# Half of the conv taps on ScalarE and GpSimd, pair sums of four heads at once, one-hot groups of 16 tokens, gate matmuls with a PSUM stride of four

## The chip, the core and the metric

The kernel runs on one core of a Trainium2 chip. Its engines have one instruction queue each and take their instructions in order: TensorE (PE, with its weight loads shown apart as PEld), VectorE (DVE), ScalarE (ACT), GpSimd (POOL) and SyncE (SP), which starts most of the transfers. They wait for one another by semaphores. The metric is the device time in microseconds, the median of the runs.

## The reference, cut to what matters

One layer with 512 tokens of width 1024. A norm and one input projection feed two groups: a conv module and differential attention with four heads. Both results are concatenated and projected out. Then each token picks experts: eight heads, each with two sets of 128 keys, of which the 16 best pairs are taken.

```python
def conv_module(cv, cg, w, b, ln_g, ln_b):
    u = cv * jax.nn.sigmoid(cg)
    y = lax.conv_general_dilated(u, w[:, None, :], window_strides=(1,),
        padding=[(CONV_KERNEL - 1, 0)], feature_group_count=CONV_WIDTH) + b   # 31 taps per channel
    return jax.nn.silu(layer_norm(y, ln_g, ln_b))

# expert choice, per token and head
sv, si = lax.top_k(s, 16)                                   # s: 8 heads x 2 x 128 key scores
cand = sv[:, :, 0, :, None] + sv[:, :, 1, None, :]
cs, ci = lax.top_k(cand.reshape(T, 8, 256), 16)
e1 = take_along_axis(si[:, :, 0], ci // 16); e2 = take_along_axis(si[:, :, 1], ci % 16)
gates = softmax(cs)
# h = gelu(x . u_tab[e1 * 128 + e2]) * gate;  y = sum of h * v_tab[e1 * 128 + e2]
```

## The kernel before

The program is one list of tile operations. A scheduler turns it into one fixed queue per engine before the run, with the waits in it; long work without a deadline (the conv taps) is set between other work of its engine. Every large product is made in three passes on PE, from a high and a low part of both operands: `split` lets ACT write the high part (`whi`, `uhi`, line 62 or 583) and DVE or POOL the remainder (`wlo` on DVE, line 63; `qlo` on POOL, line 603; `ulo` on POOL or DVE, line 584).

The stages, by the trace's times:

- To 201 us, the front. PE runs the input projections, 128 rows of weights at a time (`whi`, `wlo`), then attention in units of one head and one query tile. From a head's raw queries and keys (`qraw`, line 230 on ACT) DVE makes the rotated ones (lines 234 to 241); ACT takes the exponentials (`p`, line 257), DVE mixes the two maps (line 267). POOL takes the small rsqrt steps of three heads (lines 80 to 83, 128x4). The gated input of the conv `u` is four tiles of 128 channels and 512 tokens with 30 more columns in front. ACT writes the first tap of each (line 363), and DVE adds 30 more per tile, each one multiply and add of 128x512 (line 365, `cy<-u,convw,cy`), 120 in all. They stand between DVE's other work from 46 to 198 us. Behind them come the conv's norm and its Silu.
- 201 to 256 us: output projection, residual and second norm.
- 256 to 398 us: routing. For each head and key set a query projection, scores for three tiles of 128 tokens (TA = 384 of the 512), and `top16`, five DVE operations (lines 495 to 499). `pairs` (lines 504 to 512) adds the sorted scores of one head and one token tile, 64 and 48 candidates, and takes the `top16` of them.
- 398 to 444 us: the last of it, and the decoding of the first token tile (lines 514 on).
- 444 to 646 us: the gate stage. For each of three token tiles the choice is turned into a dense matrix of gates over 128 x 128 experts. A group of GB = 8 tokens takes a one-hot matrix `o1` of the first index and `eq` of the second (128x1024 f16 each, tokens in pairs), two products of `eq` with the high and the low part of the gates (`o`, lines 651 and 652), and for each token two matmuls that write 128 columns of a PSUM bank (line 658). ACT copies a bank with four tokens to `stage` (line 660). DVE makes `o1` (line 646), except for every third group of four, where ACT does, by eight `Abs` of 128x128 and a `Relu` (lines 640 and 642). Between the groups stand up-projections of the experts (`up`, lines 577 to 594): a load, `uhi` on ACT, `ulo` on POOL for the first 40 of them, 24 matmuls and a Gelu.
- 664 us to the end: the rest of the experts, where PE multiplies nearly without a gap, and for the last 128 tokens rows are gathered instead.

Of the kernel before, what the change touches and what calls it, by code (L numbers as in the profile page):

```python
# [34 lines left out]
GB = 8  # L35
# [5 lines left out]
FIRST, STEP = 12, 2  # L41
ACT_EVERY = 3
# [11 lines left out]
def hymba_layer(ctx: ExitStack, tc: tile.TileContext, I, out):  # L54
# [3 lines left out]
    def load(dst, src):  # L58
        nc.sync.dma_start(dst, src)
# [33 lines left out]
    # ---------------------------------------------------------------- front  # L93
# [18 lines left out]
    # the tensor engine's clock comes up, and the first table, while the first loads are on their way  # L112
# [51 lines left out]
    # 1 / rms of every token, as a column per token tile and along the free axis of all partitions  # L164
# [33 lines left out]
    lams = cload("lams", [128, 4, HD], I["lams"].to_broadcast([128, 4, HD]))  # L198
# [44 lines left out]
    # attention in units of (head, query tile), three stages apart  # L243
# [65 lines left out]
    # the layer's own embedding, projected  # L309
# [76 lines left out]
    # ------------------------------------------------- output projection, second norm  # L386
# [75 lines left out]
    # ------------------------------------------------- expert routing  # L462
# [22 lines left out]
    ne1 = rt.tile([128, NA, 128], F32, name="ne1")  # L485
# [5 lines left out]
    A.activation(irep, iota[:, :, None].to_broadcast([128, 128, 2]), AF.Copy)  # L491

# [60 lines left out]
    def decodeA(t):  # L553
# [4 lines left out]
        A.activation(ne1[:, t], tp[:, 0:128], AF.Copy, scale=-1.0)  # L558
# [37 lines left out]
    for h in range(NH):  # L596
# [18 lines left out]
        for t in range(NA):  # L615
            pairs(setA, t, h)
# [296 lines left out]
```

## Time and profile before

| | us |
|---|---|
| median of 3 runs | 1631.94 (1630.68 to 1632.47) |
| span of the profiled execution | 1628.7 |
| PE busy in the span | 1538.4 (94%) |
| PE weight loads | 1334.0 (82%) |
| DVE busy | 1296.2 (80%) |
| ACT busy | 706.2 (43%) |
| POOL busy | 537.4 (33%) |

The profiled execution's span is 3.2 us below the median. The granted clock of TensorE is 0.974 of full speed over the span. A share of the whole span is a mean over the stages above; which engine sets the end of a stage is read from the stage alone. The time of a row is that of one instruction with its own latency, so a row's mean is larger than the distance from start to start where instructions follow closely.

### The profile page before, as it was taken

The page shows a single profiled execution, that of the slowest core. Times are in us where ns is not written, and L with a number is a line of the kernel's source. Part 1 is how long each engine was busy: PE and PEld are TensorE (multiplying, and loading weights), DVE is VectorE, ACT ScalarE, POOL GpSimd, SP SyncE. Part 2 cuts the span into 40 slices and gives each one's busy share as a digit, 9 for nine tenths or more (in the row PEclk, how much of TensorE's full clock was granted, in tenths as well). Part 3 has the DMA queues.
Part 4 walks back from the last instruction along what each step waited for, and adds up shares of the span by engine and source line. Part 5 has one row for each costly group of instructions (what it writes and reads, how often), then busy time and mean ns, then how long its engine had stood idle before and what let it go on. Part 6 is the DMA issues. An engine that isn't in the chain of part 4 may idle for free. (4 is left out here: it accounts for less than half of the span.)

```text
span 1628.7 us, 22295 instructions
## 1 busy us (share of the span) xinstructions
PE 1538.4 (94%) x7945; PEld 1334.0 (82%) x7945; DVE 1296.2 (80%) x2564; ACT 706.2 (43%) x1116; POOL 537.4 (33%) x360
## 2 busy tenths in 40 slices
PE   8999898999688887999999999999999999999997
PEld 6866576888577776988888889999999999997886
DVE  4999875988989998478887888777777777777657
ACT  5434643322488796433333333333333333324432
POOL 1000103442353342244444444444444444430000
PEclk9999998999899998999999999999999999999999
DMA  7210254221234645989999999988988899977612
GB/s 241 93 66 33 74 188 154 93 85 40 78 148 169 241 179 227 316 302 355 330 351 319 347 336 351 328 325 315 330 319 319 325 320 334 328 256 258 211 44 78
DMA packets 147648, 374.83 MB, mean 230 GB/s; under 512 B 12113, under 2 KB 66129, under 8 KB 146001
## 3 DMA queue, kind: packets, MB, share of 16 engines
q1 hardware_dynamic: 110672, 239.18, 42.3%
q0 software_dynamic: 36864, 134.23, 21.9%
q8 instruction: 62, 1.02, 0.2%
q14 instruction: 50, 0.40, 0.1%
HBM read 338.76 MB, written 34.60 MB: 229 GB/s over the span
## 5 line engine op out<-in xcount | busy, mean ns | idle before, releaser
L66 PE MATMUL ups<-mTH,uhi 128*128 128x384 f32 x1024 | 354.9, 347 | 4.0 <-ACT ga L594 4.0
L68 PE MATMUL ups<-mTH,ulo 128*128 128x384 f32 x1024 | 352.9, 345 | 5.6 <-POOL ulo L584 5.6
L67 PE MATMUL ups<-mTL,uhi 128*128 128x384 f32 x1024 | 351.2, 343 | 0.0
L583 ACT ACTIVATE uhi<-uraw 128x1024 fp32r<-128x1024 f32 x128 | 135.6, 1061 | 278.6 <-PE ups L67 251.5
L718 POOL DMA_INDIRECT row<-in_u,bidx x128 | 180.1, 1407 | 224.2 <-DVE scr L722 211.4
L718 POOL DMA_INDIRECT row<-in_v,bidx x128 | 182.6, 1427 | 206.8 <-DVE acc L730 189.4
L709 PE MATMUL y<-vlo,hH 128*128 128x512 f32 x768 | 238.5, 392 | 2.0 <-DVE vlo L63 2.0
L709 PE MATMUL y<-vhi,hH 128*128 128x512 f32 x768 | 239.0, 392 | 0.3 <-ACT vhi L62 0.3
L709 PE MATMUL y<-vhi,hL 128*128 128x512 f32 x768 | 239.0, 392 | 0.0
L66 PEld LDWEIGHTS ups<-mTH,uhi 128*128 128x128 f32 x1024 | 196.6, 192 | 8.6 <-ACT ga L594 4.6
L68 PEld LDWEIGHTS ups<-mTH,ulo 128*128 128x128 f32 x1024 | 196.1, 192 | 7.0 <-POOL ulo L584 6.9
L67 PEld LDWEIGHTS ups<-mTL,uhi 128*128 128x128 f32 x1024 | 196.0, 191 | 4.9
L62 ACT ACTIVATE hH<-hf 128x384 fp32r<-128x384 f32 x128 | 67.0, 524 | 285.2 <-issue 219.3
L63 DVE TENSOR_TENSOR hL<-hf,hH 128x384 fp32r<-128x384 f32 x128 | 71.2, 557 | 146.0 <-ACT hH L62 145.8
L584 POOL TENSOR_TENSOR ulo<-uraw,uhi 128x1024 fp32r<-128x1024 f32 x40 | 123.4, 3090 | 177.3 <-ACT uhi L583 155.6
L709 PEld LDWEIGHTS y<-vlo,hH 128*128 128x128 f32 x768 | 144.0, 188 | 35.4 <-DVE vlo L63 4.0
L709 PEld LDWEIGHTS y<-vhi,hL 128*128 128x128 f32 x768 | 144.2, 188 | 31.3 <-DVE rsq L73 0.2
L722 DVE SCALAR_TENSOR_TENSOR scr<-row,mB 128x1024 f32<-128x1024 f32 x128 | 156.1, 1220 | 15.4 <-DMA row<-in_u,bidx 15.4
L709 PEld LDWEIGHTS y<-vhi,hH 128*128 128x128 f32 x768 | 143.1, 188 | 25.4 <-ACT vhi L62 1.0
L730 DVE SCALAR_TENSOR_TENSOR acc<-row,bh,acc 128x1024 f32<-128x1024 f32 x127 | 162.5, 1279 | 0.0
L63 DVE TENSOR_TENSOR vlo<-vraw,vhi 128x1024 fp32r<-128x1024 f32 x128 | 156.1, 1220 | 0.8 <-ACT vhi L62 0.8
L584 DVE TENSOR_TENSOR ulo<-uraw,uhi 128x1024 fp32r<-128x1024 f32 x88 | 107.5, 1221 | 37.2 <-ACT uhi L583 37.1
(277 smaller groups left out, 2447.9 us busy)
## 6 DMA issues: line engine op xcount, KB each, us to landing
uraw<-in_ut SPq DMA_DIRECT2D x128, 512.0 KB, 6.1
vraw<-in_v SPq DMA_DIRECT2D x128, 512.0 KB, 4.7
g_spill<-stage SPq DMA_DIRECT2D x12, 2048.0 KB, 6.9
gt<-g_spill SPq DMA_DIRECT2D x32, 768.0 KB, 9.7
qraw<-in_wq SPq DMA_DIRECT2D x16, 512.0 KB, 3.6
wraw<-in_w_in SPq DMA_DIRECT2D x15, 512.0 KB, 3.9
woraw<-in_w_out SPq DMA_DIRECT2D x8, 512.0 KB, 4.2
et<-in_wg SPq DMA_DIRECT2D x8, 512.0 KB, 4.3
```

What stands on the lines that cost most here:

```text
L62: A.activation(hi, src, AF.Copy)
L63: V.tensor_tensor(lo, src, f32(hi), op=OP.subtract)
L66: T.matmul(ps, wh, xh, start=first, stop=False)
L67: T.matmul(ps, wh, xl, start=False, stop=False)
L68: T.matmul(ps, wl, xh, start=False, stop=last)
L583: A.activation(hi, raw, AF.Copy)
L584: (P if c in first else V).tensor_tensor(lo, raw, f32(hi), op=OP.subtract)
L709: T.matmul(y[t][n], w[:, sl], x[:, n * 512:n * 512 + 512], start=c == 0 and w is hH and x is hi, stop=c == NK - 1 and l)
L718: P.indirect_dma_start(out=row, out_offset=None, in_=I["u"] if i < 128 else I["v"], in_offset=bass.IndirectOffsetOnAxis(ap=bidx[:, j:j + 1 ...
L722: tc.keep_in_program_order(V.scalar_tensor_tensor(scr, row, 1.0, mB, op0=OP.mult, op1=OP.mult, accum_out=ba[:, j:j + 1]))
L730: tc.keep_in_program_order(V.scalar_tensor_tensor(acc, row, bh[:, j:j + 1], acc, op0=OP.mult, op1=OP.add))
```

## The change

Four edits.

- Conv: the tiles are taken in the order 2, 3, 0, 1. For tiles 2 and 3 each of the 30 taps is an ACT scaling into `tap` (two buffers) and a POOL addition `cy += tap`. Tiles 0 and 1 stay on DVE.
- `pairs` is called once for four heads (HG = 4), after the fourth: two additions over four heads, 128x4x64 and 128x4x4x12, then the `top16` of each head.
- The one-hot groups have 16 tokens (GB = 16), so DVE's operations are 128x2048. Every second group has its `o1` made by a POOL subtraction, then `Abs` and `Relu` on ACT over 128x2048 each. The number of up-projections per token stays (STEP = 1).
- The gate matmuls write every fourth column of their PSUM bank (`gb[:, j::4]`), so that ACT reads the bank in order and writes runs of four elements.

```diff
-GB = 8
+GB = 16
+HG = 4
+POOL_CT = 2
-FIRST, STEP = 12, 2
-ACT_EVERY = 3
+FIRST, STEP = 12, 1
+ACT_EVERY = 2
...
-    lams = cload("lams", [128, 4, HD], I["lams"].to_broadcast([128, 4, HD]))
+    lams = inp.tile([128, S], F32, name="qraw", bufs=2)[:, 0:4 * HD].rearrange("p (a d) -> p a d", a=4)
+    load(lams, I["lams"].to_broadcast([128, 4, HD]))
...
-    for ct in range(4):
+    for ct in (2, 3, 0, 1):
         A.activation(cy[:, ct], u[:, ct, 0:S], AF.Identity, scale=convw[:, ct, 0:1], bias=convb[:, ct:ct + 1])
         for j in range(1, TAPS):
-            V.scalar_tensor_tensor(cy[:, ct], u[:, ct, j:j + S], convw[:, ct, j:j + 1], cy[:, ct], op0=OP.mult, op1=OP.add)
+            if ct < 4 - POOL_CT:
+                V.scalar_tensor_tensor(cy[:, ct], u[:, ct, j:j + S], convw[:, ct, j:j + 1], cy[:, ct], op0=OP.mult, op1=OP.add)
+            else:
+                tap = mid.tile([128, S], F32, name="tap", bufs=2)
+                A.activation(tap, u[:, ct, j:j + S], AF.Copy, scale=convw[:, ct, j:j + 1])
+                P.tensor_tensor(cy[:, ct], cy[:, ct], tap, op=OP.add)
...
-        cand = rbp.tile([128, NCAND], F32, name="cand", bufs=2)
-        V.tensor_tensor(cand[:, 0:NC0].rearrange("p (a b) -> p a b", a=4), sv[:, t, h, 0, 0:4][:, :, None].to_broadcast([128, 4, TOPK]),
-                        sv[:, t, h, 1][:, None, :].to_broadcast([128, 4, TOPK]), op=OP.add)
...
-        top16(cand, cs[:, t, h], ci[:, t, h], NCAND)
+        hs = slice(h, h + HG)
+        cand = rbp.tile([128, HG, NCAND], F32, name="cand")
+        V.tensor_tensor(cand[:, :, 0:NC0].rearrange("p h (a b) -> p h a b", a=4), sv[:, t, hs, 0, 0:4][:, :, :, None].to_broadcast([128, HG, 4, TOPK]),
+                        sv[:, t, hs, 1][:, :, None, :].to_broadcast([128, HG, 4, TOPK]), op=OP.add)
...
+        for j in range(HG):
+            top16(cand[:, j], cs[:, t, h + j], ci[:, t, h + j], NCAND)
...
-        for t in range(NA):
-            pairs(setA, t, h)
+        if h % HG == HG - 1:
+            for t in range(NA):
+                pairs(setA, t, h + 1 - HG)
...
-                if g % ACT_EVERY == ACT_EVERY - 1:
-                    ab = gst.tile([128, GB, 128], F16, name="ab", bufs=1)
-                    for j in range(GB):
-                        A.activation(ab[:, j], iota, AF.Abs, bias=ne1[:, t, tk + j:tk + j + 1])
-                    o1 = gst.tile([128, GB, 128], F16, name="o1a", bufs=1)
-                    A.activation(o1, ab, AF.Relu, bias=ones[:, 0:1], scale=-1.0)
+                if (tk // GB + t * (128 // GB)) % ACT_EVERY == ACT_EVERY - 1:
+                    o1 = gst.tile([128, GB, 128], F16, name="o1", bufs=2)
+                    P.tensor_tensor(o1, iota16[:, None, :].to_broadcast([128, GB, 128]),
+                                    e1T[:, t, tk:tk + GB][:, :, None].to_broadcast([128, GB, 128]), op=OP.subtract)
+                    A.activation(o1, o1, AF.Abs)
+                    A.activation(o1, o1, AF.Relu, bias=ones[:, 0:1], scale=-1.0)
...
-                            T.matmul(gb[:, j * 128:j * 128 + 128], o2[:, i, jj // 2, :, jj % 2], pick1[jj], start=i == 0, stop=i == 1)
+                            T.matmul(gb[:, j::4], o2[:, i, jj // 2, :, jj % 2], pick1[jj], start=i == 0, stop=i == 1)
                     t0 = g * GB + 4 * q
-                    A.activation(stage[:, :, t0:t0 + 4].rearrange("p e t -> p t e"),
-                                 gb.rearrange("p (t e) -> p t e", t=4), AF.Copy, scale=1.0 / GS)
+                    A.activation(stage[:, :, t0:t0 + 4], gb.rearrange("p (e t) -> p e t", t=4), AF.Copy, scale=1.0 / GS)
```

The lines move: in the changed program ACT's scaling is line 372, POOL's addition 373, a DVE tap 369, the exponential 260, POOL's one-hot subtraction 651, `ulo` 595, `qlo` 614.

ACT's queue before the change, from the last projections of the front to the first exponential of attention (`p`, line 257). `whi` is the high part of a weight tile, `qraw` a head's queries or keys:

```order
L62 ACTIVATE whi<-wraw 128x1024
L230 ACTIVATE qraw<-bank 128x512
L62 ACTIVATE whi<-wraw 128x1024
L230 ACTIVATE qraw<-bank 128x512
L62 ACTIVATE whi<-wraw 128x1024
L230 ACTIVATE qraw<-bank 128x512
L257 ACT_TABLE_LOAD
L257 ACTIVATE p_809,zz<-bank,nm 128x128
```

The same stretch after the change:

```order
L372 ACTIVATE tap<-u,convw 128x512 x6
L64 ACTIVATE whi<-wraw 128x1024
L233 ACTIVATE qraw<-bank 128x512
L372 ACTIVATE tap<-u,convw 128x512 x8
L233 ACTIVATE qraw<-bank 128x512
L64 ACTIVATE whi<-wraw 128x1024
L372 ACTIVATE tap<-u,convw 128x512 x8
L233 ACTIVATE qraw<-bank 128x512
L64 ACTIVATE whi<-wraw 128x1024
L372 ACTIVATE tap<-u,convw 128x512 x6
L64 ACTIVATE whi<-wraw 128x1024
L233 ACTIVATE qraw<-bank 128x512
```

Behind the last row of it stands the same table load and exponential: all 60 scalings come ahead of it. In POOL's queue the 60 additions are one row, directly ahead of the first rsqrt step.

POOL's queue before, from the last query projections into the gate stage:

```order
L603 TENSOR_TENSOR qlo<-qraw,qhi 128x1024 x3
L584 TENSOR_TENSOR ulo<-uraw,uhi 128x1024
L603 TENSOR_TENSOR qlo<-qraw,qhi 128x1024 x3
L584 TENSOR_TENSOR ulo<-uraw,uhi 128x1024 x34
L718 DMA row<-in_u,bidx 128x1024 x128
```

The same place after:

```order
L614 TENSOR_TENSOR qlo<-qraw,qhi 128x1024 x3
L595 TENSOR_TENSOR ulo<-uraw,uhi 128x1024 x8
L651 TENSOR_TENSOR o_3955<-iota_2314,e1T 128x2048
L595 TENSOR_TENSOR ulo<-uraw,uhi 128x1024 x2
L651 TENSOR_TENSOR o_4119<-iota_2314,e1T 128x2048
L595 TENSOR_TENSOR ulo<-uraw,uhi 128x1024 x2
L651 TENSOR_TENSOR o_4283<-iota_2314,e1T 128x2048
L595 TENSOR_TENSOR ulo<-uraw,uhi 128x1024 x2
```

Twelve one-hot subtractions now stand between the `ulo` of the gate stage, one for about two of them.

DVE's queue before, at the pair sums of one head (`cand`), set between the `top16` steps of the scores (`sv`, `si`) and of the sums (`cs`, `ci`):

```order
L508 TENSOR_TENSOR cand<-sv 128x64
L498 MAX sv<-tscr 128x8
L510 TENSOR_TENSOR cand<-sv 128x48
L499 MAX_INDEX si<-sv,tscr 128x8
L495 MAX cs<-cand 128x8
L508 TENSOR_TENSOR cand<-sv 128x64
L496 MAX_INDEX ci<-cs,cand 128x8
```

And after, where one such pair of additions is followed by the `top16` of four heads:

```order
L518 TENSOR_TENSOR cand<-sv 128x4x64
L507 MAX sv<-tscr 128x8
L520 TENSOR_TENSOR cand<-sv 128x4x4x12
L508 MAX_INDEX si<-sv,tscr 128x8
L504 MAX cs<-cand 128x8 x2
L505 MAX_INDEX ci<-cs,cand 128x8
L506 MATCH_REPLACE tscr<-cs,cand 128x112
L505 MAX_INDEX ci<-cs,cand 128x8
```

These blocks come twice, after heads 3 and 7, instead of after every head.

## Rows read from the trace of the kernel before

**Rows 1.** Busy time by stretches: start:end, length, busy per engine (instructions), clock, DMA, GB/s.

```profile
53.00:108.40 55.40, 55.40 (x241) 43.90 (x241) 55.12 (x80) 19.15 (x22) 0.00 (x0) 1.00 0.25 88
108.40:200.90 92.50, 81.91 (x365) 53.62 (x364) 81.89 (x177) 47.09 (x150) 9.02 (x36) 0.96 0.15 52
...
256.00:398.00 142.00, 137.04 (x681) 115.79 (x680) 114.97 (x648) 43.46 (x68) 54.77 (x24) 0.96 0.25 87
398.00:444.00 46.00, 31.27 (x166) 29.44 (x164) 46.00 (x124) 19.72 (x33) 19.81 (x8) 0.90 0.27 92
444.00:646.00 202.00, 163.04 (x1323) 149.57 (x1324) 191.91 (x379) 164.94 (x254) 81.52 (x23) 0.91 0.49 187
664.00:1628.70 964.70, 952.55 (x4670) 846.95 (x4669) 734.66 (x1016) 349.25 (x489) 362.78 (x256) 1.00 0.83 297
```

The engines in these rows are PE, PEld, DVE, ACT and POOL, in this order.

**Rows 2.** Waits: engine, tile and line, for whom, us in total, times, longest.

```profile
PE rbank L658 <- DVE o L651: 34.9, 14, 9.8
```

**Rows 3.** Timeline of DVE at 444 us: start, us, instruction.

```profile
444.17 0.68 DVE L652 TENSOR_TENSOR o<-eq,gTL 128x1024 f16<-128x1024 f16 x1
444.77 1.21 DVE L540 TENSOR_TENSOR eq<-eq,s 128x2048 f16<-128x2048 f16 x1
445.91 0.68 DVE L650 TENSOR_TENSOR eq<-irep,e2T 128x1024 f16<-128x1024 f16 x1
```

**Rows 4.** Timeline of DVE and POOL, 481 to 488 us.

```profile
481.12 8.53 POOL L584 TENSOR_TENSOR ulo<-uraw,uhi 128x1024 fp32r<-128x1024 f32 x2 [6.90 <-ACT uhi L583]
...
484.57 2.87 DVE L651 TENSOR_TENSOR o<-eq,gTH 128x1024 f16<-128x1024 f16 x1
```

**Rows 5.** Groups, whole span: operation and count, busy us, mean ns, idle before.

```profile
L603 POOL TENSOR_TENSOR qlo<-qraw,qhi 128x1024 fp32r<-128x1024 f32 x16 | 38.0, 2375 | 134.1 <-DMA qraw<-in_wq 68.3 <-ACT qhi L602 65.8
L224 ACT ACTIVATE vn<-bank,rsq 128x512 f32<-128x512 f32 x4 | 2.7, 692 | 2.3 <-PE bank L68 2.3
L510 DVE TENSOR_TENSOR cand<-sv 128x48 f32<-128x48 f32 x32 | 22.1, 692 | 0.0
```

**Rows 6.** Timeline of POOL at 167 us, during DVE taps and after them.

```profile
167.10 0.67 POOL L82 TENSOR_SCALAR rsq<-rsq 128x4 f32<-128x4 f32 x1
...
168.51 0.20 POOL L80 TENSOR_TENSOR rsq<-rsq 128x4 f32<-128x4 f32 x1
```

**Rows 7.** Groups, 444 to 646 us.

```profile
L660 ACT ACTIVATE stage<-rbank 128x512 f32<-128x512 f32 x95 | 95.0, 1135 | 35.3 <-PE rbank L658 35.2
L584 POOL TENSOR_TENSOR ulo<-uraw,uhi 128x1024 fp32r<-128x1024 f32 x23 | 81.5, 3551 | 122.0 <-ACT uhi L583 100.3 <-PE rbank L658 21.7
...
L651 DVE TENSOR_TENSOR o<-eq,gTH 128x1024 f16<-128x1024 f16 x48 | 44.8, 933 | 2.2 <-PE rbank L658 2.2
L650 DVE TENSOR_TENSOR eq<-irep,e2T 128x1024 f16<-128x1024 f16 x47 | 40.2, 856 | 0.0
L652 DVE TENSOR_TENSOR o<-eq,gTL 128x1024 f16<-128x1024 f16 x48 | 39.3, 819 | 0.0
L646 DVE TENSOR_TENSOR o1v<-irep,e1T 128x1024 f16<-128x1024 f16 x34 | 29.5, 867 | 7.4 <-PE rbank L658 7.4
```

**Rows 8.** Timeline of ACT in the front.

```profile
51.38 0.82 ACT L363 ACTIVATE cy<-u,convb,convw 128x512 f32<-128x512 f32 x1 [2.06 <-DVE u L189]
...
108.44 0.37 ACT L257 ACTIVATE p<-bank,nm 128x128 f32<-128x128 f32 x1
```

**Rows 9.** Groups of DVE, 53 to 108.4 us.

```profile
L365 DVE SCALAR_TENSOR_TENSOR cy<-u,convw,cy 128x512 f32<-128x512 f32 x52 | 35.7, 742 | 0.1
L63 DVE TENSOR_TENSOR wlo<-wraw,whi 128x1024 fp32r<-128x1024 f32 x10 | 12.2, 1215 | 0.2 <-ACT whi L62 0.2
```

**Rows 10.** Timeline of PE at 571 us, gate matmuls at full clock.

```profile
571.47 1.07 PE L658 MATMUL rbank<-o1a,o 128*128 128x128 f16 x16
572.38 1.08 PE L658 MATMUL rbank<-o1v,o 128*128 128x128 f16 x16
```

**Rows 11.** Busy time of line 658 alone, PE and PEld, 444 to 646 us.

```profile
444.00:646.00 202.00, 62.03 (x768) 49.75 (x768) 0.91 0.49 187
```

More of the change, by code (lines that the diff above doesn't have):

```diff
@@ L484, in hymba_layer @@
     A.activation(jrep, iota[:, 0:TOPK, None].to_broadcast([128, TOPK, 128]), AF.Copy)
-    ne1 = rt.tile([128, NA, 128], F32, name="ne1")
     e1T = rt.tile([128, NA, 128], F16, name="e1T")
@@ L491, in hymba_layer @@
     A.activation(irep, iota[:, :, None].to_broadcast([128, 128, 2]), AF.Copy)
+    iota16 = rt.tile([128, 128], F16, name="iota16")
+    A.activation(iota16, iota, AF.Copy)
     def top16(src, vals, idx, n):
@@ L506, in pairs @@
         sv, si, cs, ci = st
-        cand = rbp.tile([128, NCAND], F32, name="cand", bufs=2)
-        V.tensor_tensor(cand[:, 0:NC0].rearrange("p (a b) -> p a b", a=4), sv[:, t, h, 0, 0:4][:, :, None].to_broadcast([128, 4, TOPK]),
-                        sv[:, t, h, 1][:, None, :].to_broadcast([128, 4, TOPK]), op=OP.add)
-        V.tensor_tensor(cand[:, NC0:].rearrange("p (a b) -> p a b", a=12), sv[:, t, h, 0, 4:TOPK][:, :, None].to_broadcast([128, 12, 4]),
-                        sv[:, t, h, 1, 0:4][:, None, :].to_broadcast([128, 12, 4]), op=OP.add)
-        top16(cand, cs[:, t, h], ci[:, t, h], NCAND)
+        hs = slice(h, h + HG)
+        cand = rbp.tile([128, HG, NCAND], F32, name="cand")
+        V.tensor_tensor(cand[:, :, 0:NC0].rearrange("p h (a b) -> p h a b", a=4), sv[:, t, hs, 0, 0:4][:, :, :, None].to_broadcast([128, HG, 4, TOPK]),
+                        sv[:, t, hs, 1][:, :, None, :].to_broadcast([128, HG, 4, TOPK]), op=OP.add)
+        V.tensor_tensor(cand[:, :, NC0:].rearrange("p h (a b) -> p h b a", a=12), sv[:, t, hs, 0, 4:TOPK][:, :, None, :].to_broadcast([128, HG, 4, 12]),
+                        sv[:, t, hs, 1, 0:4][:, :, :, None].to_broadcast([128, HG, 4, 12]), op=OP.add)
+        for j in range(HG):
+            top16(cand[:, j], cs[:, t, h + j], ci[:, t, h + j], NCAND)
     def decode(st, t):
@@ L557, in decodeA @@
             T.transpose(tp[:, c * 128:c * 128 + 128], ef[:, c], ident)
-        A.activation(ne1[:, t], tp[:, 0:128], AF.Copy, scale=-1.0)
         A.activation(e1T[:, t], tp[:, 0:128], AF.Copy)
@@ L567, in routeB @@
                 top16(sB[:, h, c], setB[0][:, 0, h, c], setB[1][:, 0, h, c], 128)
-            pairs(setB, 0, h)
+            if h % HG == HG - 1:
+                pairs(setB, 0, h + 1 - HG)
         ef = decode(setB, 0)
@@ L614, in hymba_layer @@
                 top16(sp[:, t * 128:t * 128 + 128], setA[0][:, t, h, c], setA[1][:, t, h, c], 128)
-        for t in range(NA):
-            pairs(setA, t, h)
+        if h % HG == HG - 1:
+            for t in range(NA):
+                pairs(setA, t, h + 1 - HG)
     wqp.release()
@@ L636, in hymba_layer @@
                 it = irep[:, None].to_broadcast(sh)
-                if g % ACT_EVERY == ACT_EVERY - 1:
-                    ab = gst.tile([128, GB, 128], F16, name="ab", bufs=1)
-                    for j in range(GB):
-                        A.activation(ab[:, j], iota, AF.Abs, bias=ne1[:, t, tk + j:tk + j + 1])
-                    o1 = gst.tile([128, GB, 128], F16, name="o1a", bufs=1)
-                    A.activation(o1, ab, AF.Relu, bias=ones[:, 0:1], scale=-1.0)
+                if (tk // GB + t * (128 // GB)) % ACT_EVERY == ACT_EVERY - 1:
[4 more added lines that the diff above has]
+                    A.activation(o1, o1, AF.Relu, bias=ones[:, 0:1], scale=-1.0)
                     pick1 = [o1[:, j] for j in range(GB)]
                 else:
-                    o1 = gst.tile(sh, F16, name="o1v")
+                    o1 = gst.tile(sh, F16, name="o1", bufs=2)
                     V.tensor_tensor(o1, it, pairwise(e1T), op=OP.is_equal)
```

## The prediction

> **What bounds the kernel now.** The share of busy time over the whole span, in the table above, makes PE the bound; it is an average over stages with different limits, so I read the busy time of each engine by stretches [rows 1]. From 664 us to the end PE is busy 952.6 of 964.7 us; the change leaves the experts alone, and I cost that stretch at nothing. The change touches three earlier ones. In 53 to 108.4 us PE (55.40 of 55.40) and DVE (55.12) are both full while POOL does nothing. In 398 to 444 us DVE is full (46.0 of 46.0) and PE has holes. In 444 to 646 us, the gate stage, DVE is busy 191.9 of 202 us, PE 163, ACT 165; PE's largest wait there is for one of DVE's products, 34.9 us in 14 times [rows 2]. So DVE sets the end of the gate stage, and taking work from DVE is the right aim there. Whether it is reached depends on what POOL costs DVE.
>
> **What the trace shows of POOL beside DVE.** From 484.57 us a product of 128x1024 f16, 0.68 us alone [rows 3], takes 2.87 us, and just then POOL has two `ulo` subtractions in flight for 8.53 us [rows 4]. The product ends 2.2 us late, about what one `ulo` lasts when little hinders it (2375 ns for `qlo`, the same subtraction of the same size, [rows 5]). In the other direction POOL's operations on four elements, 0.20 us when undisturbed, take up to 0.67 beside the taps on DVE [rows 6]. I read this as: a POOL operation with two inputs and a DVE operation with two inputs from SBUF don't run at the same time, each waits for the whole of the other. I call 2.2 us per 1024 elements POOL's hold. The group means of the gate stage agree: the four DVE lines there hold 177 operations and 153.8 us [rows 7]; alone one takes 0.60 us from start to start [rows 3], so 107 us. The other 47 us are 0.92 of 23 `ulo` times 2.2 (50.6 us).
>
> **Conv taps.** DVE loses 60 of its 120 taps. They become 60 scalings on ACT and 60 additions on POOL. In ACT's queue all 60 scalings stand ahead of the first exponential and between the splits that make PE's weights; in POOL's queue the 60 additions stand in one row ahead of the small rsqrt steps of the attention heads. The `tap` tile has two buffers, so ACT can be at most two scalings ahead: ACT's queue, and with it `whi`, moves at POOL's pace. A scaling alone is about 0.69 us (the nearest row is ACT's 128x512 pass `vn`, [rows 5]), and hides behind POOL's addition. Before, ACT's first exponential starts at 108.44 us [rows 8]. After, POOL can begin at 53 us (ACT sets the third tile's first tap from 51.38 to 52.2, then comes a scaling, [rows 8]). It needs 60 x 1.1 = 66 us of hold (half of 2.2, for 512 elements); DVE has some 57 of its taps ahead of the same point, 57 x 0.67 = 38 us (a tap's 742 ns overlap the next one's start: 52 take 35.7 us of busy time), ten `wlo` at 1.2 = 12 us [rows 9], and about 4 us of rope and `u`. As these exclude one another they add: 53 + 120 = 173 us, 64 us later. If they don't exclude, POOL alone needs 60 x 1.19 = 71 us: 124 us, 16 later. So the first exponential comes late in either case; the cover that taps have now (PE busy with projections) lasts 55 us and is shorter than POOL's own work. What comes back: in 108.4 to 200.9 PE is idle 10.6 us [rows 1], partly since taps stand in DVE's queue before what attention waits for; I take 8 of it, and 3 us at the end, where the conv norm now waits for the last taps. Net **+53**, bounds +5 (16 less 11) and +64.
>
> [...]
>
> **Pairs.** 64 additions of 128x64 and 128x48 become 16 of four heads each. Those of 48 average 0.69 us and 22.1 us in all [rows 5], most of it POOL's hold, as no other operation of that size lasts so long. Up to 398 us all this lies beside PE, busy 137 of 142 us [rows 1], and costs or gains nothing. What counts is the end: pairs of heads 4 to 6 now wait for head 7. Nine calls with eight DVE instructions each, at 0.18 us (115.0 us in 648 instructions, [rows 1]), 13 us, move from the covered stretch into 398 to 444 us, where DVE is full. Against it stands the saving on the last additions and on holds that met them, up to some 13 us, of which I take 8. Net **+5**, bounds 0 and +13.
>
> **Gate stage, DVE and POOL.** Before, 36 + 3 x 48 = 180 operations of 1024; after, 12 + 3 x 24 = 84 of 2048 at 1.14 us from start to start [rows 3]. Those within the stretch go from 107 to about 93 us: -14. The other DVE work (decoding), 191.9 - 153.8 = 38 us, stays. New are 12 subtractions on POOL of 128x2048 f16. No row shows POOL on f16. Ends: by elements as `ulo`, 2 x 2.2 = 4.4 us of hold each; by bytes half, 2.2. I take 4.4: the only POOL rows there are count one element at a time and have 4-byte data. POOL's hold becomes 50.6 + 52.8 = 103 us, at 0.92 blocks DVE for 95. DVE's idle time (10 us, waits for PSUM readers among it) shrinks to 5 with fewer and larger groups. Sum: 93 + 38 + 95 + 5 = 231 us against 202, **+29**. By bytes: 93 + 38 + 71 + 5 = 207, +5. Lower end -10 (by bytes, and the halves of the block better hidden), upper +45 (the full hold, and PE's clock, 0.91 there, falling with more waiting).
>
> **Gate stage, ACT.** ACT loses eight passes of 128 and one of 1024 in each of 12 groups, and its 95 evacuations, 1135 ns each with a scattered write [rows 7], should near the 0.69 us of a plain 128x512 pass [rows 5]; it gains 24 passes over 2048. ACT was no bound (165 of 202 us); I cost its relief at nothing, since DVE covers it. `Abs` and `Relu` stand ahead of evacuations and of `uhi` in ACT's queue and wait for POOL: a late subtraction holds PE's banks up. That is inside the +45.
>
> **Gate stage, PE.** The 768 gate matmuls now write every fourth PSUM column. Nothing in this trace writes PSUM with a stride. Sixteen take 0.91 us at full clock (571.47 to 572.38, [rows 10]): 44 us in all. PE's other work is 163.0 - 62.0 = 101 us [rows 1, 11]. If a strided write doubles them, PE needs 189 us, less than 231: hidden. I take no cost, on the ground that neither end is known and DVE covers up to threefold, (231 - 101) / 43.7.
>
> [...]
>
> **Sum.** 1628.7 + 53 + 5 + 29 = 1715.7 us of span; the median of the runs lies 3.2 us above this profile's span, so **1719 us**.
>
> **Rivals.**
> A, faster: POOL's additions and subtractions don't hold DVE (`ulo` writes another type than these, so it might be a matter of that form). Front: +5. Gate: DVE 93 + 38, so PE sets the end with 163 us and some 10 of waits for ACT: -29. Pairs 0. 1628.7 - 24 + 3.2 = 1608 us. It decides from the point at which a POOL element blocks DVE for less than about a quarter of 2.2 ns, since the two stages then go from +82 to nothing. Against it: even four-element rsqrt steps of plain f32 wait for the taps [rows 6]. For it: no add of 512 or f16 subtraction is in the trace. 0.13.
> B, strided writes cost fourfold: PE needs 101 + 175 = 276 us in the gate stage, +74 in place of +29: 1628.7 + 53 + 5 + 74 + 3.2 = 1764 us. It decides from threefold on. 0.12. [...]
> C, only the front costs: the f16 subtraction goes by bytes, gate +5, 1695 us. 0.18.
> D, the front is mostly absorbed (attention's holes return all their time and DVE lets POOL through at once) and the gate neutral, 1635 to 1660: 0.05.
> The forecast itself, 1700 to 1745: 0.52.
>
> **Chances and range.** A measurement of this kernel can tell about 0.2% from no change. Faster is A and a shade of D, 0.14; within 0.2% 0.03; slower 0.83. The range runs from 1640 (D) to 1765 (B), and leaves out A and what lies above B.
>
> **What would show it.** Front: ACT's first exponential near 173 us, the 60 additions at 1.8 to 2.1 us apart in POOL's row, PE with holes between projections, and `wlo` or taps on DVE with means above 1 us. Near 124 us instead means no exclusion. Gate: DVE busy nearly all of a stretch of some 230 us with means above 2 us for its 2048-wide operations; A would have them near 1.2. Gate matmuls at 0.057 us spacing, or 0.23 under B. Pairs: after the last `top16` of head 7 twelve more before the decode of tile 0. The forecast is wrong if attention doesn't wait for that first exponential, or if PE fills the front's holes with other queued work, which its fixed order makes unlikely.

## The result

The changed kernel takes 1714.09 us (median of 4 runs, 1710.44 to 1715.41) against 1631.31 us for the kernel before on the same chip: a ratio of 1.0513, 95% interval 1.048 to 1.0546. It is slower by 5%. The forecast was 1719 us. The profiled execution has a span of 1708.2 us, 79.5 us more than before; PE is busy 1583 us of it (1538 before), DVE 1329 (1296), ACT 714 (706) and POOL 670 (537).

These are the stretches of the changed kernel that answer to [rows 1]. The columns are start:end, length, busy time of PE, PEld, DVE, ACT and POOL with the instructions, granted clock, DMA share and GB/s. The borders are the first exponential, the first lower weight part (`woL`) of the output projection, the last query projection copied out by ACT, the first gate matmul, the last evacuation of a gate bank and the first matmul of the experts' second product:

```profile
53.00:166.50 113.50, 70.70 (x249) 52.84 (x247) 113.27 (x77) 59.80 (x83) 98.80 (x60) 0.80 0.14 45
166.50:256.60 90.10, 78.67 (x362) 52.19 (x361) 51.48 (x124) 48.46 (x151) 7.58 (x36) 0.96 0.16 53
...
449.60:504.90 55.30, 39.13 (x208) 37.93 (x208) 52.85 (x179) 19.94 (x28) 25.05 (x9) 0.87 0.23 74
504.90:729.40 224.50, 197.07 (x1313) 188.13 (x1314) 218.70 (x308) 134.50 (x177) 111.30 (x34) 0.93 0.46 166
749.50:1708.20 958.70, 946.74 (x4641) 842.52 (x4639) 732.04 (x1009) 346.25 (x485) 362.46 (x256) 1.00 0.84 297
```

The same marks in both traces tell where the 79.5 us come from:

| mark (us) | before | after | later by |
|---|---|---|---|
| first exponential | 108.4 | 166.5 | 58.1 |
| output projection begins | 200.9 | 256.6 | 55.7 |
| last query projection copied | 393.6 | 449.6 | 56.0 |
| first gate matmul | 444.3 | 504.9 | 60.6 |
| last gate bank evacuated | 647.4 | 729.4 | 82.0 |
| experts' second product begins | 669.1 | 749.5 | 80.4 |
| end of the span | 1628.7 | 1708.2 | 79.5 |

So the front costs 56 us, the stage before the gates 4.6, the gate stage 21.4, and 2.5 come back later.

**The front.** Groups of the stretch before the first exponential: operation and count, busy us, mean ns, idle time before with its releasers.

```profile
L373 POOL TENSOR_TENSOR cy<-cy,tap 128x512 f32<-128x512 f32 x60 | 98.8, 1647 | 55.8 <-ACT tap L372 51.5
L369 DVE SCALAR_TENSOR_TENSOR cy<-u,convw,cy 128x512 f32<-128x512 f32 x53 | 84.0, 1635 | 0.2
L372 ACT ACTIVATE tap<-u,convw 128x512 f32<-128x512 f32 x60 | 42.8, 721 | 44.5 <-POOL cy L373 44.4
L70 PE MATMUL bank<-aH,wlo 128*128 128x512 f32 x43 | 19.7, 458 | 24.3 <-DVE wlo L65 24.3
...
L65 DVE TENSOR_TENSOR wlo<-wraw,whi 128x1024 fp32r<-128x1024 f32 x9 | 17.8, 1983 | 0.0
```

A DVE tap took 742 ns before [rows 9] and takes 1635 now; the lower weight parts take 1983 instead of 1215, and PE waits 24.3 us for them in this one row. A few instructions show how it runs (timeline: start, us, instruction):

```profile
78.51 13.94 POOL L373 TENSOR_TENSOR cy<-cy,tap 128x512 f32<-128x512 f32 x8
...
82.25 2.28 DVE L65 TENSOR_TENSOR wlo<-wraw,whi 128x1024 fp32r<-128x1024 f32 x1
83.48 0.72 ACT L372 ACTIVATE tap<-u,convw 128x512 f32<-128x512 f32 x1 [0.95 <-POOL cy L373]
84.45 8.54 DVE L369 SCALAR_TENSOR_TENSOR cy<-u,convw,cy 128x512 f32<-128x512 f32 x5
...
84.58 0.79 PE L69 MATMUL bank<-wlo,aH 128*128 128x512 f32 x1 [6.74 <-DVE wlo L65]
```

Five DVE taps fill 8.54 us, 1.71 each, and eight POOL additions 13.94, 1.74 each: one of each in turn. Of 1.71 us a tap alone needs 0.66 (before the change six follow one another in 3.98 us, from 62.30 to 66.28), so an addition holds DVE for 1.05. ACT's scaling (0.72 us) mostly waits 0.95 for POOL, and PE stands still for 6.74 us in this place.

Not every DVE instruction is held. Two that run while POOL makes a row of eight additions:

```profile
59.62 13.65 POOL L373 TENSOR_TENSOR cy<-cy,tap 128x512 f32<-128x512 f32 x8 [0.97 <-ACT tap L372]
...
68.18 0.68 DVE L190 TENSOR_TENSOR cvr<-bank,r 128x512 f32<-128x512 f32 x1
70.38 1.76 DVE L191 TENSOR_TENSOR u<-cvr,sg 128x512 f32<-128x512 f32 x1
```

Before the change both took 0.68 us. The first has one of its two inputs in PSUM (`bank`) and still takes 0.68; the second has both in SBUF and ends 1.08 us late.

**The gate stage.** Groups from the first gate matmul to the last evacuation, to hold against [rows 7]:

```profile
L670 PE MATMUL rbank<-o,o 128*128 128x128 f16 x768 | 99.0, 332 | 25.0 <-DVE o L663 21.6 <-DVE o L664 2.6 <-ACT o L654 0.6
L595 POOL TENSOR_TENSOR ulo<-uraw,uhi 128x1024 fp32r<-128x1024 f32 x23 | 65.9, 2875 | 105.2 <-ACT uhi L594 79.8 <-PE ups L70 15.1 <-PE rbank L670 7.4
L672 ACT ACTIVATE stage<-rbank 128x512 f32<-128x512 f32 x96 | 53.8, 607 | 31.9 <-PE rbank L670 31.8
L651 POOL TENSOR_TENSOR o<-iota,e1T 128x2048 f16<-128x2048 f16 x11 | 45.8, 4164 | 9.6 <-PE rbank L670 6.5 <-ACT e1T L569 3.1
L663 DVE TENSOR_TENSOR o<-eq,gTH 128x2048 f16<-128x2048 f16 x23 | 41.3, 1795 | 0.0
...
L653 ACT ACTIVATE o<-o 128x2048 f16<-128x2048 f16 x11 | 21.0, 1910 | 51.3 <-POOL o L651 51.3
```

DVE's operations of 2048 average 1.5 to 1.8 us where one took 1.21 before [rows 3]; the evacuation falls from 1135 to 607 ns; the gate matmuls are busy 99 us against 62 [rows 11].

### The profile page after: what moved, and what is told of

Same layout as the page of the kernel before. It is cut to its first block, busy times and chain, and to the rows that moved or that the text cites. A ratio compares the mean times of both kernels' runs of the same rounds, so it can differ in the third digit from the quotient of the medians.

```text
span 1708.2 us, 22209 instructions
## 1 busy us (share of the span) xinstructions
PE 1583.4 (93%) x7945; PEld 1381.0 (81%) x7945; DVE 1328.5 (78%) x2360; ACT 714.0 (42%) x1090; POOL 669.8 (39%) x432
## 3 DMA queue, kind: packets, MB, share of 16 engines
q8 instruction: 62, 1.02, 0.2%
## 5 line engine op out<-in xcount | busy, mean ns | idle before, releaser
L729 POOL DMA_INDIRECT row<-in_u,bidx x128 | 180.6, 1411 | 224.5 <-DVE scr L733 209.6
L595 POOL TENSOR_TENSOR ulo<-uraw,uhi 128x1024 fp32r<-128x1024 f32 x40 | 108.1, 2710 | 159.3 <-ACT uhi L594 133.8
L64 ACT ACTIVATE vhi<-vraw 128x1024 fp32r<-128x1024 f32 x128 | 135.4, 1058 | 0.0
```

The lines of the kernel that those rows point to most:

```text
L64: A.activation(hi, src, AF.Copy)
L595: (P if c in first else V).tensor_tensor(lo, raw, f32(hi), op=OP.subtract)
L729: P.indirect_dma_start(out=row, out_offset=None, in_=I["u"] if i < 128 else I["v"], in_offset=bass.IndirectOffsetOnAxis(ap=bidx[:, j:j + 1 ...
```

## Experiments

All ratios are to the kernel before, run on the same chip. The kernel before has medians from 1626.9 to 1631.3 us in the four sets of runs, so a difference in us between runs of different sets can be off by some 4 us; the ratios are the safer guide there.

**One: the taps back on DVE.**

```diff
-POOL_CT = 2
+POOL_CT = 0
-    for ct in (2, 3, 0, 1):
+    for ct in range(4):
```

> The changed kernel with all 120 taps back on DVE; the other three edits stay. Exclusion theory (a two-input operation on POOL and one on DVE never run together, so POOL's 60 additions lengthen the front by their own time): the first exponential returns from 166 to about 108 us and the time falls by 53 to 58 us, to 1656 to 1661 us. Rival (the front is late for another reason, such as the moved load of lams or scalings in ACT's way): a fall of clearly under 50 us.

Measured: 1658.07 us, ratio 1.0174 (1.0148 to 1.02). The first exponential starts at 109.0 us and the output projection at 200.2. The conv edit alone costs 56 us, and nothing else makes the front late.

**Two: one tile on ACT and POOL.**

```diff
-POOL_CT = 2
+POOL_CT = 1
-    for ct in (2, 3, 0, 1):
+    for ct in (3, 0, 1, 2):
```

> The changed kernel with one tile's 30 taps on ACT and POOL instead of two. Exclusion: the half dose costs about half, 30 additions of 0.9 to 1.1 us of hold each: first exponential at 134 to 141 us, 26 to 33 us more than with all taps on DVE, 1684 to 1692 us. Rival (no exclusion, POOL was just too slow for its 60 additions): 30 x 1.29 = 39 us end inside the 55 us in which PE projects, so nothing is left of the loss, 1656 to 1661 us.

Measured: 1688.31 us, ratio 1.0358 (1.0332 to 1.0384), 30 us more than with all taps on DVE. ACT in the front:

```profile
141.14 0.37 ACT L260 ACTIVATE p<-bank,nm 128x128 f32<-128x128 f32 x1 [0.30 <-DVE nm L258]
```

The exponential is 32 us later for 30 additions, 1.07 us each. The price goes with the number of additions; had POOL merely been too slow, these thirty would have ended under cover by the sum above (39 of 55 us, at 1.29 each; the shortest of the changed kernel's sixty took 1295 ns).

**Three: the scalings stay on ACT, the additions go to DVE.**

```diff
-                P.tensor_tensor(cy[:, ct], cy[:, ct], tap, op=OP.add)
+                V.tensor_tensor(cy[:, ct], cy[:, ct], tap, op=OP.add)
```

> The changed kernel with the 60 scalings still on ACT, and the 60 additions on DVE instead of POOL. Exclusion: DVE has as many operations as before the change, POOL none, so the front is back within 5 us, 1652 to 1664 us. Rival (ACT's scalings ahead of the weight splits and of the first exponential are the cause): 30 scalings still stand there, at 0.7 us each some 16 to 20 us of the loss remain, 1674 us or more.

Measured: 1657.14 us, ratio 1.0164 (1.0138 to 1.0191). Its groups up to the first exponential (112.2 us):

```profile
L372 ACT ACTIVATE tap<-u,convw 128x512 f32<-128x512 f32 x31 | 21.7, 719 | 11.7 <-DVE cy L373 11.7
L373 DVE TENSOR_TENSOR cy<-cy,tap 128x512 f32<-128x512 f32 x31 | 21.1, 683 | 0.1
L369 DVE SCALAR_TENSOR_TENSOR cy<-u,convw,cy 128x512 f32<-128x512 f32 x26 | 18.9, 743 | 0.0
```

Thirty-one scalings still stand ahead of the exponential, and the time is that of the first experiment within 1 us. The output projection begins at 206.8 us instead of 200.2 with all taps on DVE, so at most 7 us of the front's 56 can lie with ACT's scalings, and they don't show in the end. ACT's queue is not the main cause; without POOL the operations on DVE are back at 683 and 743 ns.

**Four: the one-hot matrix of every group on DVE.**

```diff
-                if (tk // GB + t * (128 // GB)) % ACT_EVERY == ACT_EVERY - 1:
+                if (tk // GB + t * (128 // GB)) % ACT_EVERY == ACT_EVERY:
```

> The changed kernel with the one-hot matrix of all 24 groups on DVE; no subtraction on POOL and no Abs and Relu behind it. Exclusion: DVE gets 12 x 1.14 = 14 us more of its own and loses some 45 us of blocking, 107 + 38 + 47 + 5 = 197 us; PE, busy 196.5 of 223.9 us after the change, is then level, so the gate stage lasts about 205 us and the time falls by 15 to 25 us, to 1690 to 1699 us. Rival (POOL relieves DVE as meant): 14 us slower, 1728 us.

Measured: 1689.4 us, ratio 1.0367 (1.0342 to 1.0391), 24 to 25 us faster than the changed kernel, at the upper end of what was expected. The stage before the gates and the gate stage:

```profile
452.00:503.70 51.70, 38.02 (x208) 36.84 (x209) 50.18 (x179) 18.03 (x26) 21.50 (x8) 0.90 0.24 80
503.70:710.20 206.50, 190.82 (x1329) 183.53 (x1330) 188.66 (x301) 93.73 (x154) 63.81 (x22) 0.95 0.48 180
```

DVE takes over twelve more operations and is busy 189 us instead of 219. The gate stage gives back 18 us, and the stage ahead of it 3.6.

**Five: rows of 128 PSUM columns, and the scattered evacuation.**

```diff
-                            T.matmul(gb[:, j::4], ...
+                            T.matmul(gb[:, j * 128:j * 128 + 128], ...
-                    A.activation(stage[:, :, t0:t0 + 4], gb.rearrange("p (e t) -> p e t", t=4), ...
+                    A.activation(stage[:, :, t0:t0 + 4].rearrange("p e t -> p t e"),
+                                 gb.rearrange("p (t e) -> p t e", t=4), ...
```

> The changed kernel with gate matmuls that write 128 neighbouring PSUM columns, and the scattered write of the evacuation as before. Matmul busy time on this line falls from 99 to about 62 us and ACT's evacuation rises from 607 to 1135 ns. Exclusion theory (DVE with POOL sets the end of the gate stage, the doubled matmuls are hidden): 0 to 8 us faster, 1706 to 1714 us. Rival (PE sets the end since its writes have a stride): 20 to 37 us faster, 1677 to 1694 us.

Measured: 1726.3 us, ratio 1.0578 (1.0558 to 1.0597): 11 to 12 us slower than the changed kernel, a miss of both expectations. Its gate stage:

```profile
L672 ACT ACTIVATE stage<-rbank 128x512 f32<-128x512 f32 x96 | 92.5, 1135 | 5.7 <-PE rbank L670 5.7
L595 POOL TENSOR_TENSOR ulo<-uraw,uhi 128x1024 fp32r<-128x1024 f32 x23 | 87.6, 3820 | 99.8 <-ACT uhi L594 66.1 <-PE rbank L670 24.4 <-PE ups L70 7.4
...
L70 PE MATMUL ups<-mTH,ulo 128*128 128x384 f32 x181 | 68.8, 380 | 39.3 <-POOL ulo L595 39.3
L670 PE MATMUL rbank<-o,o 128*128 128x128 f16 x768 | 54.9, 233 | 28.5 <-ACT o L654 15.7 <-DVE o L663 11.6 <-DVE o L664 0.6
```

The matmuls are back at 54.9 us, but PE now waits 39.3 us for `ulo` and 15.7 for ACT's `Relu`. My reading: in the changed kernel POOL, ACT and PE wait in a ring (POOL's `ulo` for ACT's `uhi`, ACT's `Abs` for POOL's subtraction, PE for both), and 40 us more of evacuation in ACT's queue lengthens it. Two things are undone at once here, the stride and the cheap evacuation, and they pull in opposite directions. Experiment nine tries the ring.

**Six: pair sums of one head.**

```diff
-HG = 4
+HG = 1
-        cand = rbp.tile([128, HG, NCAND], F32, name="cand")
+        cand = rbp.tile([128, HG, NCAND], F32, name="cand", bufs=2)
```

> The changed kernel with pair sums of one head at a time again. If the moved top16 of heads 4 to 6 cost the stage before the gates 5 us: the first gate matmul 4 to 5 us earlier and the time about 1709 us. Rival (the joint additions save DVE time that counts): 3 to 8 us slower.

Measured: 1725.48 us, ratio 1.0579 (1.0561 to 1.0597), 11 us slower, more than either expectation. The profile doesn't put these where either theory does:

```profile
455.00:510.60 55.60, 37.71 (x205) 35.89 (x205) 54.07 (x144) 21.50 (x28) 23.77 (x9) 0.90 0.22 76
510.60:743.30 232.70, 193.82 (x1317) 184.72 (x1318) 203.69 (x283) 131.44 (x176) 122.16 (x34) 0.93 0.42 157
```

The stage before the gates lasts as long as with joint pairs (55.6 and 55.3). The gate stage is 8 us longer though DVE is busy 15 us less, while PE waits 19.9 us for `ulo` instead of 8.2. The scheduler sets ACT's rows there in another order, so this looks like the ring again; which link of it costs the 8 us stays open.

**Seven: the kernel before, with `ulo` on DVE.**

```diff
-        (P if c in first else V).tensor_tensor(lo, raw, f32(hi), op=OP.subtract)
+        V.tensor_tensor(lo, raw, f32(hi), op=OP.subtract)
```

> The kernel before, with the 40 ulo subtractions of POOL on DVE. Exclusion: in the gate stage DVE gets 23 x 1.13 = 26 us of its own and loses 47 us of blocking: 107 + 38 + 26 + 10 = 181 instead of 202 us; in 398 to 444 us 8 x 1.13 = 9 us take the place of some 15. Together 22 to 28 us faster than before, 1604 to 1610 us. Rival (no exclusion, DVE is full and gets more to do): 20 to 35 us slower.

Measured: 1586.77 us, ratio 0.9729 (0.9713 to 0.9746). It beats both kernels by 44 and 127 us, and more than expected. The same two stages (50.7 and 203.1 us in the kernel before):

```profile
395.00:433.90 38.90, 36.11 (x200) 35.09 (x200) 36.76 (x128) 20.65 (x37) 0.00 (x0) 0.96 0.28 96
433.90:607.40 173.50, 160.52 (x1373) 143.18 (x1374) 159.80 (x303) 165.28 (x256) 0.00 (x0) 0.99 0.59 224
```

DVE gets 32 operations more in the two and is busy 160 us instead of 192 in the second; PE is now level with 160.5 of 173.5 us, at a clock of 0.99 instead of 0.91 [rows 1]. Some of DVE's fall is only moved: about a hundred small instructions now stand behind the gate stage, before the experts' second product (first row of seven, then of the kernel before):

```profile
607.40:626.50 19.10, 16.10 (x93) 15.46 (x91) 18.69 (x100) 7.03 (x11) 0.00 (x0) 1.00 0.94 341
...
647.40:669.10 21.70, 21.70 (x117) 21.70 (x117) 6.50 (x10) 8.66 (x13) 7.06 (x4) 0.94 0.76 277
```

Over the three stages DVE is busy 215 us instead of 248, with more work than before. POOL's subtractions blocked it for longer than they take on DVE itself: 25 `ulo` are 30.5 us of DVE's busy time in the second stage, 1.22 each, where the product beside a `ulo` of POOL's ended 2.2 us late [rows 3, 4].

**Eight: the same with groups of 16, a quarter of the one-hot matrices on ACT.**

```diff
-GB = 8
+GB = 16
-FIRST, STEP = 12, 2
-ACT_EVERY = 3
+FIRST, STEP = 12, 1
+ACT_EVERY = 4
-                if g % ACT_EVERY == ACT_EVERY - 1:
-                    ab = gst.tile([128, GB, 128], F16, name="ab", bufs=1)
+                if (tk // GB + t * (128 // GB)) % ACT_EVERY == ACT_EVERY - 1:
+                    o1 = gst.tile([128, GB, 128], F16, name="o1")
```

> The kernel before, with all ulo subtractions on DVE, groups of 16 tokens, every fourth group's one-hot matrix by 16 Abs and a Relu on ACT (the same share as before), rows of 128 columns in PSUM. Exclusion: DVE's gate stage 90 operations of 1.14 us (100 in the stretch) + 38 + 26 + 5 = 169 us, so PE with 163 us becomes level: the stage about 172 to 176 us and the time 30 to 36 us under the kernel before, 1596 to 1602 us. Rival: as for the run without groups of 16, slower than before.

Measured: 1608.82 us, ratio 0.986 (0.9842 to 0.9877). It is faster than before, but 22 us slower than experiment seven and 7 us above the 1596 to 1602 us expected. Its largest wait of PE from the first gate matmul on (engine, tile, for whom: us, times, longest):

```profile
PE ups L66 <- ACT uhi L583: 21.4, 6, 6.0
```

One group's one-hot matrix is now 16 `Abs` of 0.4 us and a `Relu` of 2.0 in ACT's queue, and `uhi` stands behind. DVE is busy only 158 of the gate stage's 185 us, so it isn't the limit. My reading is that the same share of ACT's work in larger lumps made PE wait; no run changes the lumps alone.

**Nine: four and five together.**

> The changed kernel with all one-hot matrices on DVE and rows of 128 columns in PSUM (the two edits that were undone alone at 1689 and 1726 us). Ring theory (with the one-hot chain on POOL and ACT, ACT's longer evacuation delays what POOL and PE wait for; without that chain ACT has room): PE has 38 us less, DVE with ulo's blocking sets the end, 0 to 8 us faster than with the one-hot on DVE alone, 1681 to 1690 us. Rival (a scattered evacuation costs in any case): 8 to 15 us slower than that, 1697 to 1704 us.

Measured: 1681.7 us, ratio 1.0333 (1.0315 to 1.0351), 8 us faster than experiment four by the medians and 5 to 6 by the ratios, as the ring theory expected.

```profile
503.40:697.90 194.50, 158.65 (x1332) 148.48 (x1332) 190.52 (x305) 131.53 (x154) 64.09 (x22) 0.94 0.51 192
```

The evacuation is as long as in experiment five (1158 ns), and here it doesn't eat up the gain: without the one-hot chain through POOL and ACT the cheaper matmuls shorten the gate stage by 12 us. That speaks for the ring, without showing which of its waits costs what.

**Ten: experiment seven with pair sums of four heads.**

```diff
-        for t in range(NA):
-            pairs(setA, t, h)
+        if h % HG == HG - 1:
+            for t in range(NA):
+                pairs(setA, t, h + 1 - HG)
```

> The kernel before with ulo on DVE, and pair sums of four heads at once. If pairs by one head cost 11 us after the change only by the order on POOL's and ACT's queues: within 5 us of the same kernel with single pairs, 1582 to 1592 us. Rival (the 48 additions saved are DVE time that counts): 6 to 11 us faster, 1576 to 1581 us.

Measured: 1597.47 us, ratio 0.9806 (0.9785 to 0.9827): 11 us slower than with single pairs, a miss of both.

```profile
395.50:443.80 48.30, 41.05 (x214) 38.76 (x215) 45.10 (x193) 19.19 (x33) 0.00 (x0) 0.93 0.23 77
443.80:617.30 173.50, 160.40 (x1359) 141.36 (x1360) 162.67 (x309) 166.79 (x260) 0.00 (x0) 0.98 0.59 224
```

The gate stage is the same to the tenth (173.5), and the stage ahead of it 9.4 us longer, with 193 DVE instructions in place of 128. DVE is busy 8.3 us longer there. That is the price of moving the `top16` of heads 4 to 6 behind the last scores.

**Eleven and twelve: the changed kernel with nothing of the change's work on POOL, nor `ulo`, with the stride and with rows.** Taps, one-hot matrices and `ulo` are on DVE, by the edits of one, four and seven; twelve has that of five too.

> The changed kernel with taps, one-hot matrices and ulo all on DVE: groups of 16, joint pairs and the stride of four stay. DVE's gate stage is 107 + 38 + 26 = 171 us, PE's 99 + 97 = 196 us, so the doubled gate matmuls are bare for the first time: stage 198 to 205 us, 1612 to 1620 us. Rival (the stride is hidden here too): as the kernel before with ulo on DVE, 1587 us or less.

> The same with rows of 128 columns in PSUM. PE has 157 us, DVE 171 us: the stage 176 to 182 us, 1590 to 1598 us, 18 to 28 us faster than with the stride. Rival (the evacuation with scattered writes, 1135 instead of 607 ns, costs more than the stride): slower than with the stride.

Measured: 1621.44 us with the stride (ratio 0.996, 0.9945 to 0.9974) and 1595.21 with rows (0.9805, 0.9783 to 0.9827). Gate stage with the stride:

```profile
446.50:632.50 186.00, 181.45 (x1304) 173.25 (x1304) 158.30 (x216) 92.32 (x149) 0.00 (x0) 0.98 0.54 204
```

And with rows:

```profile
445.80:607.20 161.40, 149.75 (x1319) 139.67 (x1319) 158.17 (x218) 127.57 (x149) 0.00 (x0) 0.97 0.64 236
```

The stage with the stride was expected at 198 to 205 us and the time at 1612 to 1620; with rows, 176 to 182 and 1590 to 1598. So both stages are 12 us or more shorter than DVE's and PE's sums said, and one of the times lies just outside its range. With the stride PE is busy in all but 4.5 us of the stage; rows shorten it by 24.6, with the dearer evacuation that goes with them. Here the price of the stride is bare. With rows, groups of 16 with the one-hot matrix on DVE have the shortest gate stage of all (161.4 against 173.5 in experiment seven); what the kernel loses against seven lies in the stage ahead (49.5 us against 38.9, with the joint pairs) and in 7 us of the experts' part, whose cause I leave open. Groups of 16, rows and single pairs without POOL weren't tried.

## Why the prediction was right

**Exclusion of POOL and DVE** was the step that carried the forecast, and it held: taps and additions alternate, at 1.05 us of hold per addition of 512, the loss goes with the number of additions (1.07 us for each of thirty, experiments one and two), it vanishes when the same additions run on DVE (three, where the taps take 743 ns again), and work taken off POOL and given to a full DVE makes DVE less busy in the gate stage (189 us instead of 219 in four, 160 instead of 192 in seven). What in the two engines makes them exclude one another isn't shown.

One reading behind it was neater than its rows. The prediction sets 0.60 us from start to start against durations, which overlap their neighbours, and finds 47 us of hold in the four DVE lines of the gate stage. In seven, with nothing on POOL, these lines last 0.68 us each, such as

```profile
L651 DVE TENSOR_TENSOR o<-eq,gTH 128x1024 f16<-128x1024 f16 x47 | 32.0, 682 | 0.0
```

So some 33 of the 153.8 us are hold and not 47; the rest would have to lie in the decoding, whose 38 us were taken as plain work. The agreement with 0.92 of 23 times 2.2 says less than it seems to.

**Conv taps, +53:** measured +55.7. The parts were less exact. The first exponential came at 166.5 us, not 173: 58.1 us late instead of 64. And of the 11 us that were to come back only 2.4 did: attention's stretch lasts 90.1 us instead of 92.5, though DVE has 30 us less to do in it. So taking the taps out of attention's way was oversized by about 9 us, and the delay by 6 (53 taps and nine lower weight parts stand ahead of it, not 57 and ten, and an addition holds DVE for 1.05 us, not 1.1). That the sum is within 3 us is luck: the two errors have opposite signs.

**Pairs, +5:** the stage before the gates grew by 4.6 us, but the number is right by luck; the step that failed is the cause. Undoing the joint pairs leaves the stage at 55.6 us (six). Most of it is the one-hot edit: without POOL's subtraction the stage takes 51.7 (four), against 50.7 before the change. The timeline of the changed kernel ahead of its first gate matmul:

```profile
494.76 4.59 POOL L651 TENSOR_TENSOR o<-iota,e1T 128x2048 f16<-128x2048 f16 x1
...
495.80 4.62 DVE L662 TENSOR_TENSOR eq<-irep,e2T 128x2048 f16<-128x2048 f16 x1
500.35 3.36 DVE L551 TENSOR_TENSOR eq<-eq,s 128x2048 f16<-128x2048 f16 x1
```

The first group's `eq` takes 4.62 us instead of 1.21, beside the first subtraction. The two effects that the prediction weighed under pairs exist: without POOL the moved `top16` cost 9.4 us (ten; the estimate was 13). With POOL the joint pairs cost the stage nothing (55.3 us against 55.6 in six), where I had counted 8 of up to 13 as coming back; that the saved holds are what came back isn't shown.

**Gate stage, +29:** measured +21.4. The term that was most open, POOL's subtraction of 2048 f16 elements, was oversized. Its twelve rows have a median of 4.46 us, close to the 4.4 chosen, but most of them contain a wait for DVE. Three of them, with what DVE does beside them:

```profile
519.87 4.34 POOL L651 TENSOR_TENSOR o<-iota,e1T 128x2048 f16<-128x2048 f16 x1 [4.01 <-PE rbank L670]
520.67 3.67 DVE L542 CAST dc<-iu 128x128 f32<-128x128 uint32 x1
...
533.30 3.59 POOL L651 TENSOR_TENSOR o<-iota,e1T 128x2048 f16<-128x2048 f16 x1
533.35 4.64 DVE L663 TENSOR_TENSOR o<-eq,gTH 128x2048 f16<-128x2048 f16 x1
...
572.71 3.60 POOL L651 TENSOR_TENSOR o<-iota,e1T 128x2048 f16<-128x2048 f16 x1 [3.10 <-ACT e1T L569]
572.95 0.28 DVE L507 MAX8 sv<-tscr 128x8 f32<-128x128 f32 x1
```

Where POOL starts first, or DVE only sorts (`MAX8`, 0.28 us here as elsewhere), the subtraction lasts 3.6 us, and the product beside it takes 4.64 us instead of 1.21: 3.4 us of hold. That lies between the two ends, 4.4 by elements and 2.2 by bytes. The total is about 8 us lower than the account; DVE's busy time, 218.7 us, is 7 us under the 226 of the sum (231 less 5 idle). By estimate, eleven subtractions of 3.4 us in the stage and 23 `ulo` of 2.2 make 88 us of hold instead of 103: at the prediction's 0.92 the sum falls to 217 us, and charged in full it is 224, where the stage measured 224.5. So the share 0.92 looks too small and the 4.4 too large, and the two partly cancel. Rival C fell all the same: at half price the stage would have grown by 5 us only. The sign that was named, means above 2 us for DVE's operations of 2048, didn't come (1.5 to 1.8 us), since part of the hold falls on the decoding; a `CAST` there takes 3.67 us instead of 0.27.

**ACT's relief, costed at nothing:** this step was wrong. Undoing the cheap evacuation costs the changed kernel 11 to 12 us, although the matmuls get 44 us cheaper with it (five). My reading is that ACT stands in the chain of the one-hot groups that the change itself made; nine supports it, since without that chain the dear evacuation costs less than the cheaper matmuls gain. DVE was not the only cover.

**The stride, hidden up to threefold:** the factor is 1.9. At full clock before, 16 gate matmuls took 0.91 us [rows 10]. After, 32 take 3.43 us to the start of the next instruction, at a clock of 1.00 too:

```profile
669.47 3.67 PE L670 MATMUL rbank<-o,o 128*128 128x128 f16 x32
672.90 0.42 PE L68 MATMUL ups<-mTH,uhi 128*128 128x384 f32 x1
```

That is 0.107 us each instead of 0.057. Rival B, which needed threefold, fell. PE then stands at 197 of 224.5 us, little below DVE. That the stride was hidden in the changed kernel isn't shown, as no run undoes it alone; without the one-hot chain it shows by 12 us in the gate stage (nine against four), and once POOL is out of the way by 24.6.

**Rival A** (no exclusion, 1608 us) fell with experiments one to four, and D with the front's 56 us. The sum had 1715.7 us for the span and the trace has 1708.2: front and pairs came out 2.6 us over the account together, the gate stage 7.6 under, and 2.5 us came back behind it. The exclusion was right; the closeness of the total, 5 us, owes something to errors that cancel.

## What to carry to other kernels

An idle POOL was not free help for a full DVE here: where DVE's work is of the kind that was held (two inputs from SBUF, and the casts of the decoding), price POOL's operation as DVE time, at what it held DVE for (1.05 us per addition of 512, 3.4 per f16 subtraction of 2048, where operations of that size take DVE 0.68 and 1.21 undisturbed). DVE work that reads PSUM or sorts was not held here (0.68 and 0.28 us beside POOL) and is the first to try there. Look in the trace for DVE operations that last several times their usual mean beside a POOL operation. Ask first whether work that is on POOL already should come back: here the smallest edit of all, 40 subtractions moved from POOL to the engine that looked full, was worth 44 us. And fewer, larger instructions may not help where something urgent queues behind them: in experiment eight PE waited 21.4 us for `uhi`, and the time was 22 us longer than in seven.

## What the runs showed of the hardware

- The shortest POOL subtraction of f16 took 3.6 us for 2048 elements (4.46 in the median of twelve, most with a wait for DVE); the f32 one took 2375 ns for 1024 [rows 5]. Half the bytes save a quarter of the time per element here (1.76 ns against 2.32), not half. The two differ in their operands too: the f16 one repeats both of its inputs.
- Beside POOL's work, DVE operations with both inputs in SBUF ended late by most of POOL's duration: 1.08 us beside additions of 512, whose shortest took 1.30, and 3.4 beside a subtraction of 2048 that took 3.6. One with an input in PSUM kept its 0.68 us and a `MAX8` its 0.28 (0.30 at most in 64), while a `CAST` with a single input went from 0.27 to 3.67.
- Matmuls of 128 columns that write every fourth f32 column of a PSUM bank took 1.9 times as long from start to start as those that write neighbouring columns (0.107 against 0.057 us), and the loads of their weights had a median of 135 ns against 97 (experiments eleven and twelve).
- An ACT evacuation of 128x512 f32 took 607 ns in the mean when it read the bank in order and wrote runs of four elements, 1135 when it wrote single elements apart [rows 7].
- TensorE's granted clock, as a mean over a stage, was lower where PE had holes: 0.80 in the changed front, where PE is busy 71 of 113.5 us (1.00 before, busy throughout), and 0.99 in experiment seven's gate stage (busy 160.5 of 173.5) against 0.91 in the kernel before (163.0 of 202 [rows 1]).
